# Scan tables of a two-layer trunk: complex products in three double-width VectorE steps, parameters of both layers made together early in layer 0

## The chip, the cores and the metric

The kernel runs on one core of a Trainium2 chip. The metric is the device time of one execution in microseconds (us); the median of several executions stands for a kernel. The engines are PE (TensorE, matrix products), DVE (VectorE), ACT (ScalarE), POOL (GpSimd) and SP (SyncE, which here issues most of the transfers). Each works through its own instructions in the order in which they were emitted, and waits at an instruction until what it needs is there.

## The reference, cut to what matters

The trunk has two layers over 256 latent and 256 context tokens of width 1024. Each layer mixes tokens through four parallel branches (multi-head latent attention, neighbourhood attention, an S5 scan, a Mamba-2 scan), merges them with gates, projects the sum, and then runs a mixture of 16 experts. The change concerns the S5 branch alone:

```python
def s5_scan(abar, bbar, u, h0, reverse):
    bu = jnp.einsum('gpc,btgc->btgp', bbar, u.astype(jnp.complex64))
    a = jnp.broadcast_to(abar, bu.shape)
    a_cum, h = lax.associative_scan(_linear_combine, (a, bu), reverse=reverse, axis=1)
    return h + a_cum * h0[:, None]
...
    for d, rev in ((0, False), (1, True)):
        a = lax.complex(a_re[d].astype(f32), a_im[d].astype(f32))
        abar = jnp.exp(jnp.exp(log_step[d].astype(f32))[:, None] * a)
        bbar = ((abar - 1.0) / a)[:, :, None] * lax.complex(b_re[d].astype(f32), b_im[d].astype(f32))
        cm = lax.complex(c_re[d].astype(f32), c_im[d].astype(f32))
        h_ctx = s5_scan(abar, bbar, uc, h_zero, rev)
        h_lat = s5_scan(abar, bbar, ul, h_ctx[:, 0] if rev else h_ctx[:, -1], rev)
        y_lat = y_lat + readout(cm, h_lat)
```

`abar`, `bbar` and `cm` depend on weights alone. The kernel turns them into tables: powers of `abar` times `bbar` (the input table), `cm` times powers of `abar` (the readout table), a kernel of short convolutions made from both, and powers of the rotation of `abar` over longer distances. The scan itself then consists of matrix products with these tables.

## The kernel before

The class `Trunk` runs `mix_phase` (L860) and then the expert phase, for layer 0 and then for layer 1. All products of activations and weights go through PE with each operand split in two parts (high and low), which makes three matmuls of each (L256 to L258). A weight arrives in `unit` (L361): SP issues the transfer into a slot of a ring `w` (two slots in the token mixing of layer 0), ACT makes the high part `wh` (L341), and DVE, for some units POOL, makes the low part `wl` (L342). SP issues in order, so a transfer whose slot is not free holds back those behind it.

Two streams of work are woven into the branches. `ada` (L446 to L474) makes the modulation of later stages from conditioning weights: SP loads tiles `wa` (four slots), PE multiplies (L454), DVE adds into `R` (L458), PE transposes `R` (L466). `merge` makes the gates and the merged stream `yT` (DVE at L1512 or L1521 and L1522, behind PE's products).

The tables of a layer are made in `s5_tables` (L690), a generator whose steps are emitted in turn with steps of `merge` by `together` (L938): for layer 0 in layer 0's token mixing after the neighbourhood attention, for layer 1 also in layer 0, after the S5 branch, just ahead of the projection. All of it happens in the first third of the run. The tables go to DRAM and are read back by the branch.

`s5_tables` first makes the parameters of its layer from 128x16 arrays: loads of `a` and the step sizes on ACT's queue, an exact exponential (`exp_exact`, L311), cosine and sine, nine powers `pw`, the factor `f`, and eight squarings `ro` of the rotation. Then for each half `h` of the groups: `bb` (128x128 twice), the input table `IT` in two parts of 128x4x128, each with real and imaginary part, the readout table `CP` in two parts of 128x4x144, PE transposes of `IT` (L822), a block diagonal `BD`, the PE products of `CP` and `BD` (L837), their copies `Kc`, and six doublings of `W` from 128x8 to 128x256 columns. The temporary tiles are named `t5...`, those of a complex product `cm1` to `cm4`.

Every complex product goes through `cmul` (L666): DVE makes four of the six steps (L683 to L686), POOL the other two (L687 and L688), the second of which needs DVE's L686.

What sets the order around the change is the order of emission, sorted by priorities: `first()` and `urgent()` raise the transfers and the splits of weights.

Of the kernel before, what the change touches and what calls it, by code (L numbers as in the profile page):

```python
# [12 lines left out]
F32 = mybir.dt.float32  # L13
# [3 lines left out]
OP = mybir.AluOpType  # L17
# [4 lines left out]
DEPTH = 2  # L22
# [168 lines left out]
class Trunk:  # L191
# [477 lines left out]
    def cmul(self, ore, oim, ar, ai, br, bi, shape, tag, pool, conj=False, im=None):  # L669

        nc = self.nc
        n = int(np.prod(shape))
        ar2, ai2 = im or (ar, ai)

        def tmp(s):
            x = self.sb([128, n], f"cm{s}", F32, pool)
            names = "abcd"[:len(shape)]
            if len(shape) == 1:
                return x
            return x.rearrange("p (" + " ".join(names) + ") -> p " + " ".join(names), **dict(zip(names, shape)))  # L680

        t1, t2, t3, t4 = tmp(1), tmp(2), tmp(3), tmp(4)
# [7 lines left out]
    def s5_tables(self, l):  # L690

        nc, t, wk = self.nc, self.t, self.ar
        dr = self.dr
        dt = lambda s, shape: dr.tile(shape, F32, name=f"s5{s}{l}", tag=f"s5{s}{l}")
        T = self.tabs[l] = {
            "IN": dt("in", [2, 128, 16 * 128]), "CP": dt("cp", [2, 128, 2 * 8 * 9 * 16]),
            "K": dt("k", [256, 240]), "W": dt("w", [2, 128, 2 * 8 * 64]),
            "R": dt("r", [128, 16]),
        }
        v = lambda s, shape=(128, 16): self.sb(list(shape), "t5" + s, pool=wk)  # L700
        a = v("a", (128, 2, 16))
        nc.scalar.dma_start(a, t["s5a"][l])
        x0 = v("x0")
# [12 lines left out]
        k, r, sn, sh, cm1, cs = v("k"), v("r"), v("sn"), v("sh"), v("cm1"), v("cs")  # L716
# [11 lines left out]

        pw = v("pw", (128, 2, 9, 16))
# [5 lines left out]
        def cm(o, i, j, b, tag):  # L735
            n = j - i
            bb = [pw[:, z, b, :][:, None, :].to_broadcast([128, n, 16]) for z in (0, 1)]
            self.cmul(pw[:, 0, o:o + n, :], pw[:, 1, o:o + n, :], pw[:, 0, i:j, :], pw[:, 1, i:j, :],
                      bb[0], bb[1], (n, 16), tag, wk)
        cm(2, 1, 2, 1, "p1")  # L740
        cm(3, 1, 3, 2, "p2")
        cm(5, 1, 5, 4, "p4")

        nre, f, dn, q1, q2 = v("nre"), v("f", (128, 2, 16)), v("dn"), v("q1"), v("q2")
# [10 lines left out]
        nc.vector.tensor_mul(f[:, 0, :], q1, dn)  # L755
# [9 lines left out]
        nc.scalar.dma_start(T["R"], R8)  # L765
        ro = v("ro", (128, 2, 9, 16))
        nc.vector.tensor_copy(ro[:, 0, 0, :], cs)
        nc.vector.tensor_copy(ro[:, 1, 0, :], sn)
        yield
        for j in range(1, 9):  # L770
            a_ = [ro[:, z, j - 1, :] for z in (0, 1)]
            self.cmul(ro[:, 0, j, :], ro[:, 1, j, :], a_[0], a_[1], a_[0], a_[1], (16,), "ro", wk)

        yield
        for h in range(2):
            qs = slice(h * 8, h * 8 + 8)
            b = v("b", (128, 2, 8, 16))
            c = v("c", (128, 2, 8, 16))
            nc.scalar.dma_start(b, t["s5b"][l, h])
            nc.scalar.dma_start(c, t["s5c"][l, h])  # L780
            cn = v("cn", (128, 2, 8, 16))
            nc.vector.tensor_scalar(cn, c, -1.0, None, OP.mult)
            bb = v("bb", (128, 2, 8, 16))
            fb = [f[:, z, qs][:, :, None].to_broadcast([128, 8, 16]) for z in (0, 1)]
            self.cmul(bb[:, 0], bb[:, 1], b[:, 0], b[:, 1], fb[0], fb[1], (8, 16), "bb", wk)

            pq = v("pq", (128, 2, 8, 9))
            for z in range(2):
                nc.vector.tensor_copy(pq[:, z], pw[:, z, :, qs].rearrange("p k q -> p q k"))
            yield  # L790

            IT = [v(f"IT{z}", (128, 8, 128)) for z in (0, 1)]
            for d in range(2):
                dq = lambda z: z.rearrange("p (g d) x -> p g d x", d=2)[:, :, d, :]
                po = []
                for z in range(2):
                    p_ = dq(pq[:, z])
                    p_ = p_[:, :, 7::-1] if d == 0 else p_[:, :, 0:8]
                    po.append(p_[:, :, :, None].to_broadcast([128, 4, 8, 16]))
                o = [dq(IT[z]).rearrange("p g (s c) -> p g s c", s=8) for z in (0, 1)]  # L800
                bs = [dq(bb[:, z])[:, :, None, :].to_broadcast([128, 4, 8, 16]) for z in (0, 1)]
                self.cmul(o[0], o[1], bs[0], bs[1], po[0], po[1], (4, 8, 16), "it", wk)
                yield

            CP = v("CP", (128, 2, 8, 9, 16))
            for d in range(2):
                dq = lambda z: z.rearrange("p (g d) x -> p g d x", d=2)[:, :, d, :]
                po = []
                for z in range(2):
                    p_ = dq(pq[:, z])  # L810
                    p_ = p_[:, :, 8::-1] if d == 1 else p_
                    po.append(p_[:, :, :, None].to_broadcast([128, 4, 9, 16]))
                o = [CP[:, z].rearrange("p (g d) i c -> p g d i c", d=2)[:, :, d] for z in (0, 1)]
                cc = [dq(y[:, z])[:, :, None, :].to_broadcast([128, 4, 9, 16]) for y in (c, cn) for z in (0, 1)]
                self.cmul(o[0], o[1], cc[0], cc[1], po[0], po[1], (4, 9, 16), "cp", wk, im=cc[2:])
                yield
            IN = v("IN", (128, 16, 128))
            for q4 in range(4):
                ps = self.psum("sm")
                for j in range(4):  # L820
                    q, z = divmod(q4 * 4 + j, 2)
                    nc.tensor.transpose(ps[:, j * 128:(j + 1) * 128], IT[z][:, q, :], self.ident)  # L822
                self.copy(IN[:, q4 * 4:(q4 + 1) * 4, :].rearrange("p a b -> p (a b)"), ps, eng=self.on("IN"))
            nc.scalar.dma_start(T["IN"][h], IN.rearrange("p a b -> p (a b)"))
            nc.scalar.dma_start(T["CP"][h], CP.rearrange("p z q i c -> p (z q i c)"))

            BD = v("BD", (128, 2, 8, 32))
            nc.gpsimd.memset(BD, 0.0)
            for g2 in range(2):
                self.copy(BD[g2 * 64:(g2 + 1) * 64, :, :, g2 * 16:(g2 + 1) * 16], bb[g2 * 64:(g2 + 1) * 64], eng=self.on("BD"))  # L830
            yield
            ps = self.psum("sm")
            for d in range(2):
                for g in range(4):
                    q = g * 2 + d
                    for z in range(2):
                        nc.tensor.matmul(ps[g * 32:(g + 1) * 32, d * 128:(d + 1) * 128], BD[:, z, q, :],  # L837
                                         CP[:, z, q, d:d + 8, :].rearrange("p i c -> p (i c)"),
                                         start=z == 0, stop=z == 1, tile_position=(0, g * 32))
# [9 lines left out]
            W = v("W", (128, 2, 8, 64))  # L849
            nc.vector.memset(W[:, 0, :, 0:1], 1.0)  # L850
            nc.vector.memset(W[:, 1, :, 0:1], 0.0)
            for j in range(6):
                n = 1 << j
                rb = [ro[:, z, 3 + j, qs][:, :, None].to_broadcast([128, 8, n]) for z in (0, 1)]
                self.cmul(W[:, 0, :, n:2 * n], W[:, 1, :, n:2 * n], W[:, 0, :, 0:n], W[:, 1, :, 0:n],
                          rb[0], rb[1], (8, n), f"w{j}", wk)
# [4 lines left out]
    def mix_phase(self, l):  # L861
        nc, t, tc = self.nc, self.t, self.tc
        with ExitStack() as es:
# [4 lines left out]
            side = dict(e=front, side="right") if l else dict(e=front)  # L868
# [1242 lines left out]
```

## Time and profile before

| | us |
|---|---|
| median of 3 runs | 1989.41 |
| the 3 runs | 1983.79 to 1990.79 |
| the profiled execution | 1984.16 |
| its span in the profile | 1982.4 |
| PE busy in it | 1691.3 |
| VectorE busy in it | 854.3 |
| GpSimd busy in it | 347.7 |

The profile is of one execution. Its busy times are summed over a run whose stages differ: in layer 0 the token mixing lasts from 0 to about 640 us, then come the experts until about 1110 us, then the same for layer 1. So a share of the whole span says little; the stretches in which the tables are made have to be read by themselves.

### The profile page before, as it was taken

To read this page: it belongs to the slowest core of one execution; us is meant where nothing else is said; L and a number is where in the kernel's file an instruction comes from. 1 tells how busy PE (TensorE), PEld (TensorE's weight loads), DVE (VectorE), ACT (ScalarE), POOL (GpSimd) and SP (SyncE) were. 2 spreads that over 40 slices of the span, in tenths; PEclk is the share of its full clock that TensorE was granted. 3 is DMA by queue.
4 is the path that set the end of the run, shared out by engine and by line. 5 is a ranking of instruction groups with operands and counts; after the bars stand their busy time and mean duration, and the time that the engine had idled before them with its cause. 6 is when DMAs were issued, how large, how long until landed. Compare 5 with 4: busy or idle time off the path is not lost.

```text
span 1982.4 us, 28289 instructions
## 1 busy us (share of the span) xinstructions
PE 1691.3 (85%) x11294; PEld 1031.6 (52%) x11294; DVE 854.3 (43%) x1866; ACT 499.4 (25%) x982; POOL 347.7 (18%) x463
## 2 busy tenths in 40 slices
PE   6999988999889799999888879889897766766765
PEld 2676666666668543434232259868895432322322
DVE  2357698557896521212121156567974110100102
ACT  5422423322324311101010164344352110000001
POOL 3231154234450000000000051333500000000000
PEclk9999999999999899999999989999997886776777
DMA  8747367274248699999999843435568999999996
GB/s 286 256 164 240 107 226 263 91 224 149 89 170 318 259 407 419 419 420 420 419 419 420 359 171 106 117 99 169 182 241 333 421 420 419 420 420 420 420 419 264
DMA packets 106735, 574.04 MB, mean 290 GB/s; under 512 B 13580, under 2 KB 17484, under 8 KB 55404
## 3 DMA queue, kind: packets, MB, share of 16 engines
q1 hardware_dynamic: 95052, 533.77, 69.2%
q0 software_dynamic: 5616, 20.52, 3.4%
q10 hardware_dynamic: 5936, 17.95, 2.4%
q8 instruction: 89, 1.46, 0.3%
q14 instruction: 42, 0.34, 0.1%
HBM read 556.47 MB, written 15.71 MB: 289 GB/s over the span
## 4 chain that ended last, share of the span: by engine, by line
PE 49%; DMA 32%; DVE 12%; ACT 2%; issue 2%; POOL 2%; SPq 0%; DVEq 0%; ACTq 0%; POOLq 0%
DMA w<-in_w_down_dram 11%; DMA w<-in_w_gate_dram 9%; DMA w<-in_w_up_dram 9%; PE psmm L1945 8%; PE psmm L256 7%; PE psmm L258 6%; PE psmm L257 6%; PE psmm L1974 4%; PE psbg L454 2%; DVE wl L342 2%; PE pssm L1847 1%; DMA wa<-in_w_ada_dram 1%; PE pssm L1993 1%; PE pssm L1012 1%; PE pssm L257 1%
## 5 line engine op out<-in xcount | busy, mean ns | idle before, releaser
L1945 PE MATMUL psmm<-w,xs 128*32 128x256 f32 (+1 forms) x3072 | 406.8, 527 | 101.2 <-DMA w<-in_w_up_dram 52.9
L1945 PEld LDWEIGHTS psmm<-w,xs 128*32 128x32 f32 (+1 forms) x3072 | 140.7, 133 | 355.1 <-issue 176.8
L258 PE MATMUL psmm<-hT,wl 128*128 128x512 f32 (+1 forms) x672 | 237.9, 354 | 4.4 <-DVE wl L342 4.3
L256 PE MATMUL psmm<-hT,wh 128*128 128x512 f32 (+1 forms) x672 | 241.3, 359 | 0.2 <-ACT wh L341 0.2
L257 PE MATMUL psmm<-hT,wh 128*128 128x512 f32 (+1 forms) x672 | 237.1, 353 | 0.0
L1974 PE MATMUL psmm<-w,aT 128*32 128x256 f32 (+1 forms) x1536 | 202.4, 521 | 37.3 <-DMA w<-in_w_down_dram 23.5
L341 ACT ACTIVATE wh<-w 128x1024 fp32r<-128x1024 f32 (+1 forms) x128 | 144.8, 1137 | 184.9 <-PE psmm L258 51.4
L342 DVE TENSOR_TENSOR wl<-w,wh 128x1024 fp32r<-128x1024 f32 (+1 forms) x101 | 139.7, 1390 | 55.7 <-ACT wh L341 55.5
L1974 PEld LDWEIGHTS psmm<-w,aT 128*32 128x32 f32 (+1 forms) x1536 | 69.4, 134 | 161.3 <-issue 80.4
L256 PEld LDWEIGHTS psmm<-hT,wh 128*128 128x128 f32 x672 | 128.3, 191 | 41.5 <-issue 20.6
L258 PEld LDWEIGHTS psmm<-hT,wl 128*128 128x128 f32 x672 | 128.2, 191 | 22.5 <-DVE wl L342 5.0
L257 PEld LDWEIGHTS psmm<-hT,wh 128*128 128x128 f32 x672 | 128.5, 191 | 18.2 <-issue 2.2
L244 DVE COPY YS<-psmm 32x512 f32<-32x512 f32 (+1 forms) x64 | 35.7, 558 | 234.6 <-PE psmm L1974 234.1
L1953 DVE SCALAR_TENSOR_TENSOR th<-th,psmm 128x512 f32<-128x512 f32 (+1 forms) x32 | 17.7, 555 | 225.5 <-ACT th L1952 225.5
L1954 DVE TENSOR_TENSOR th<-th,psmm 128x512 f32<-128x512 f32 (+1 forms) x32 | 17.7, 555 | 224.0 <-PE psmm L1945 224.0
L1804 POOL COPY sel<-cst 32x128 f32<-32x128 f32 (+1 forms) x24 | 6.8, 284 | 611.3 <-DVE GT L1812 576.4
L236 ACT ACTIVATE YS<-psmm 32x512 f32<-32x512 f32 (+1 forms) x64 | 30.7, 479 | 322.9 <-PE psmm L1974 322.4
L342 POOL TENSOR_TENSOR wl<-w,wh 128x1024 fp32r<-128x1024 f32 (+1 forms) x27 | 69.8, 2586 | 233.0 <-ACT wh L341 212.4
L258 PE MATMUL psmm<-wh,hT 128*128 128x256 f32 x288 | 83.6, 292 | 5.0 <-POOL hT L584 4.5
L256 PE MATMUL psmm<-wh,hT 128*128 128x256 f32 x288 | 84.0, 292 | 1.8 <-ACT hT L582 1.8
L257 PE MATMUL psmm<-wl,hT 128*128 128x256 f32 x288 | 82.7, 288 | 0.0
L1952 ACT ACTIVATE th<-psmm 128x512 f32<-128x512 f32 (+1 forms) x32 | 15.7, 490 | 212.2 <-PE psmm L1945 212.2
(533 smaller groups left out, 2721.3 us busy)
## 6 DMA issues: line engine op xcount, KB each, us to landing
w<-in_w_gate_dram SPq DMA_DIRECT2D x128, 1024.0 KB, 19.9
w<-in_w_up_dram SPq DMA_DIRECT2D x128, 1024.0 KB, 19.9
w<-in_w_down_dram SPq DMA_DIRECT2D x128, 1024.0 KB, 19.9
wa<-in_w_ada_dram SPq DMA_DIRECT2D x96, 512.0 KB, 5.8
w<-in_w_gb_dram SPq DMA_DIRECT2D x48, 640.0 KB, 4.2
w<-in_w_in_dram SPq DMA_DIRECT2D x40, 512.0 KB, 3.7
w<-in_w_gb_dram SPq DMA_DIRECT2D x20, 512.0 KB, 4.3
w<-in_w_out_dram SPq DMA_DIRECT2D x20, 512.0 KB, 5.0
```

The lines of the kernel that those rows point to most:

```text
L236: nc.scalar.activation(out, in_, AF.Copy)
L244: nc.vector.tensor_copy(out, in_)
L256: nc.tensor.matmul(out, lh, rh, start=start, stop=False)
L257: nc.tensor.matmul(out, lh, rl, start=False, stop=False)
L258: nc.tensor.matmul(out, ll, rh, start=False, stop=stop)
L341: nc.scalar.activation(hi, x, AF.Copy)
L342: (eng or nc.vector).tensor_tensor(lo, x, hi.bitcast(F32), OP.subtract)
L454: nc.tensor.matmul(ps[q:q + 32, :], self.sc[:, k].rearrange("p a b -> p (a b)"), w[:, j * 512:(j + 1) * 512], start=k == 0, stop=k == 7, t ...
L1012: nc.tensor.matmul(ps[:, :nk * 128], q(h, tt), k(h, nk * 128), start=True, stop=True)
L1847: nc.tensor.matmul(ps[:, kk, s, :n], self.x[2 * s + i][:, (k + kk) * 128:(k + kk + 1) * 128], oh[:, s, i], start=i == 0, stop=i == 1)
L1945: nc.tensor.matmul(ps[j * M:(j + 1) * M, :N], xs[:, k, e4].rearrange("p s c -> p (s c)"), w[:, kk, j * N:(j + 1) * N], start=n + kk == 0, ...
L1974: nc.tensor.matmul(bank(j)[j * M:(j + 1) * M, :N], aT[:, b, hf, :], w[:, kk, j * N:(j + 1) * N], start=k == 0, stop=k == 7, tile_position= ...
```

## The change

A new generator `tables_begin` makes the parameters of both layers at once, as arrays of 128x32. Its loads stand on SP's queue, and its steps are emitted right after `start`, which makes the first normalised activations `hT` of layer 0. Powers, rotations and the factor stay in SBUF in tiles `pw`, `ro` and `fb` of the pool `ap`.

`cmul` gives way to `product`: three DVE steps over real and imaginary part together (two products and a sum), so that `IT` and `CP` are made in steps of 128x1024 and 128x1152 columns. The operands for it, with negated and doubled parts, are made by copies on ACT, and the first part of `c` is loaded a second time. POOL keeps only the memset of `BD`.

```diff
-    def cmul(self, ore, oim, ar, ai, br, bi, shape, tag, pool, conj=False, im=None):
...
-        nc.vector.tensor_tensor(t1, ar, br, OP.mult)
-        nc.vector.tensor_tensor(t2, ai, bi, OP.mult)
-        nc.vector.tensor_tensor(ore, t1, t2, OP.add if conj else OP.subtract)
-        nc.vector.tensor_tensor(t3, ar2, bi, OP.mult)
-        nc.gpsimd.tensor_tensor(t4, ai2, br, OP.mult)
-        nc.gpsimd.tensor_tensor(oim, t4, t3, OP.subtract if conj else OP.add)
...
+    def tables_begin(self, es):
...
+        n = 16 * DEPTH
...
+        self.pw = self.ap.tile([128, 2, 9, n], F32, name="t5pw")
+        self.ro = self.ap.tile([128, 2, 6, n], F32, name="t5ro")
+        self.fb = self.ap.tile([128, 2, n], F32, name="t5f")
...
+        yield
+        nc.sync.dma_start(a.rearrange("p z (l q) -> p z l q", l=DEPTH), t["s5a"].rearrange("l p z q -> p z l q"))
         for g2 in range(2):
-            nc.scalar.dma_start(x0[g2 * 64:(g2 + 1) * 64, :], t["s5ls"][l, g2].partition_broadcast(64))
-        step = self.exp_exact(x0, 16, wk)
+            nc.sync.dma_start(x0[g2 * 64:(g2 + 1) * 64, :].rearrange("p (l q) -> p l q", l=DEPTH),
+                                t["s5ls"][:, g2].partition_broadcast(64))
+        step = self.exp_exact(x0, n, wk)
...
+    def product(self, out, a, b, tmp):
+
+        nc = self.nc
+        nc.vector.tensor_tensor(out, a[0], b[0], OP.mult)
+        nc.vector.tensor_tensor(tmp, a[1], b[1], OP.mult)
+        nc.vector.tensor_tensor(out, out, tmp, OP.add)
...
+            nc.scalar.dma_start(c[:, 0:2], t["s5c"][l, h])
+            nc.scalar.dma_start(c[:, 2], t["s5c"][l, h][:, 0])
+
+            self.copy(c[:, 1:3], c[:, 1:3], scale=-1.0, eng="act")
...
+            self.copy(bb[:, 0], bb[:, 2], scale=-1.0, eng="act")
...
+                self.product(dq(IT, d).rearrange("p q (s c) -> p q s c", s=8), bs, p_, tm()[:, :, 0:8])
                 yield
...
+                self.product(dq(CP, d).rearrange("p q (i c) -> p q i c", c=16), cc, p_, tm())
                 yield
...
+                begun = ExitStack()
+                begin = self.tables_begin(begun)
+                next(begin)
                 arena(self.start, hT)
+                for _ in begin:
+                    pass
+                begun.close()
```

On DVE's queue early in the run, between the last low parts of `hT` (L584) and the convolution blocks of the Mamba-2 branch (`cvu`, `cv`; L1165 and L1169, after the change L1177 and L1181), there stands before the change one split of a weight:

```order
48 L584 TENSOR_TENSOR hT_0_90<-hf_375,hT_0_89 128x256
49 L584 TENSOR_TENSOR hT_0_90<-hf_379,hT_0_89 128x256
50 L342 TENSOR_TENSOR wl_606<-w_603,wh_605 128x1024
51 L1165 SCALAR_TENSOR_TENSOR cvu_548<-psmm_523,cwh_504,cvu_548 128x2x254
52 L1165 SCALAR_TENSOR_TENSOR cvu_548<-psmm_523,cwh_504,cvu_548 128x2x255 x2
53 L1169 SCALAR_TENSOR_TENSOR cv_506<-cvt_553,cvu_548 128x512
```

After it, the last `hT` is row 63, and rows 64 to 141 lie between it and the first `cvu`. Here are the last of them:

```order
136 L761 TENSOR_TENSOR t5ro<-t5ca_117_532 128x32
137 L760 TENSOR_TENSOR t5ro<-t5ca_117_532,t5q_100_454 128x32
138 L758 TENSOR_TENSOR t5ca_118_537<-t5ro 128x64
139 L759 TENSOR_TENSOR t5q_100_454<-t5ro 128x32
140 L761 TENSOR_TENSOR t5ro<-t5ca_118_537 128x32
141 L760 TENSOR_TENSOR t5ro<-t5ca_118_537,t5q_100_454 128x32
142 L1177 SCALAR_TENSOR_TENSOR cvu_707<-psmm_682,cwh_663,cvu_707 128x2x254
```

77 steps of the parameters and one split (row 83) moved in between the activations and the first convolution block. A further 13 parameter steps stand ahead of the last `hT`, at rows 47 to 59.

On SP's queue in the same place, the loads of the parameters moved in behind the second unit of the input projection. Before:

```order
19 L368 DMA w_447<-in_w_in_dram 128x1024
20 L368 DMA w_517<-in_w_in_dram 128x1024
21 L901 DMA cstm_91<-in_cstm_dram 128x844
22 L446 DMA wa_509<-in_w_ada_dram 128x1024
23 L368 DMA w_564<-in_w_in_dram 128x1024
```

After:

```order
20 L368 DMA w_676<-in_w_in_dram 128x1024
21 L689 DMA t5a_126<-in_s5a_dram 128x4x16
22 L691 DMA t5x_6_127<-in_s5ls_dram 64x2x16 x2
23 L913 DMA cstm_91<-in_cstm_dram 128x844
24 L368 DMA w_723<-in_w_in_dram 128x1024
25 L446 DMA wa_668<-in_w_ada_dram 128x1024
26 L368 DMA w_762<-in_w_in_dram 128x1024
```

Three small transfers went in, and a unit `w` now stands ahead of the first tile `wa`.

On DVE's queue in the first table stretch, the step that adds into `R` (L458), for which PE waits, stands before the change behind the products for `IT` and some of those for `CP`:

```order
358 L683 TENSOR_TENSOR cm_502_2480<-t5bb_2373,t5pq_2384 128x512
359 L684 TENSOR_TENSOR cm_503_2481<-t5bb_2373,t5pq_2384 128x512
360 L342 TENSOR_TENSOR wl_2700<-w_2697,wh_2699 128x1024
361 L685 TENSOR_TENSOR t5IT_490_2428<-cm_502_2480,cm_503_2481 128x4x128
362 L686 TENSOR_TENSOR cm_515_2533<-t5cn_2371,t5pq_2384 128x576
363 L683 TENSOR_TENSOR cm_513_2531<-t5c_2368,t5pq_2384 128x576
364 L684 TENSOR_TENSOR cm_514_2532<-t5c_2368,t5pq_2384 128x576
365 L458 TENSOR_TENSOR R_1620<-R_1620,psbg_1621 128x512
```

After it, it stands behind both products for `IT` (rows 345 to 348, 351 and 353), both for `CP` (the last step is row 364), and the first doublings of `W`:

```order
364 L768 TENSOR_TENSOR t5CP_2397<-t5CP_2397,t5tm_2442 128x8x144
365 L768 TENSOR_TENSOR t5W_2616<-t5W_2616,t5tw_2619 128x16x2
366 L768 TENSOR_TENSOR t5bb_2669<-t5bb_2669,t5tb_2670 128x256
367 L766 TENSOR_TENSOR t5W_2616<-t5W_2616,t5ro 128x16x4
368 L767 TENSOR_TENSOR t5tw_2627<-t5W_2616,t5rn_2272 128x16x4
369 L342 TENSOR_TENSOR wl_2684<-w_2681,wh_2683 128x1024
370 L768 TENSOR_TENSOR t5W_2616<-t5W_2616,t5tw_2627 128x16x4
371 L766 TENSOR_TENSOR t5W_2616<-t5W_2616,t5ro 128x16x8
372 L767 TENSOR_TENSOR t5tw_2631<-t5W_2616,t5rn_2272 128x16x8
373 L458 TENSOR_TENSOR R_1779<-R_1779,psbg_1780 128x512
```

No step of the parameters stands in this stretch any more; the tables' first step comes right behind the tail of the neighbourhood attention, at row 340.

## Rows read from the trace of the kernel before

**Rows 1.** The page: busy time by engine; shares of the chain that ended last.
```profile
PE 1691.3 (85%) x11294; PEld 1031.6 (52%) x11294; DVE 854.3 (43%) x1866; ACT 499.4 (25%) x982; POOL 347.7 (18%) x463
...
PE 49%; DMA 32%; DVE 12%; ACT 2%; issue 2%; POOL 2%; SPq 0%; DVEq 0%; ACTq 0%; POOLq 0%
```

**Rows 2.** Busy time by stretch: us, PE, PEld, DVE, ACT, POOL, PEclk, DMA share, GB/s.
```profile
50.00:100.00 50.00, 49.23 (x239) 32.72 (x238) 19.66 (x25) 20.95 (x31) 14.43 (x8) 1.00 0.74 258
240.00:263.00 23.00, 23.00 (x121) 15.36 (x118) 16.70 (x107) 8.45 (x13) 6.71 (x23) 1.00 0.55 173
263.00:327.00 64.00, 51.01 (x337) 38.39 (x336) 59.73 (x115) 14.58 (x21) 39.91 (x44) 0.89 0.63 222
498.00:522.00 24.00, 24.00 (x108) 18.90 (x103) 20.50 (x113) 10.01 (x14) 7.81 (x24) 1.00 0.33 107
522.00:592.00 70.00, 54.74 (x283) 40.83 (x283) 67.65 (x121) 15.91 (x24) 45.20 (x46) 0.98 0.38 139
700.00:1100.00 400.00, 368.66 (x1765) 142.24 (x1764) 76.11 (x132) 51.53 (x102) 3.98 (x14) 1.00 1.01 418
```

**Rows 3.** PE's waits from 263 to 327, longest groups: waiter, releaser, total, times, longest.
```profile
PE psbg L466 <- DVE R L458: 6.7, 1, 6.7
PE pssm L822 <- POOL t5IT L688: 2.7, 1, 2.7
PE pssm L822 <- DVE t5IT L685: 1.8, 1, 1.8
```

**Rows 4.** PE's waits from 522 to 592, the longest groups.
```profile
PE pssm L822 <- DVE t5IT L685: 5.7, 4, 2.5
PE pssm L837 <- DVE t5CP L685: 3.2, 3, 2.0
PE pssm L822 <- POOL t5IT L688: 3.2, 4, 0.8
```

**Rows 5.** Groups by line and shape from 263 to 327 (busy us, mean ns | idle before).
```profile
L684 DVE TENSOR_TENSOR cm<-t5bb,t5pq 128x512 f32<-128x512 f32 x4 | 4.7, 1170 | 0.0
...
L683 DVE TENSOR_TENSOR cm<-t5bb,t5pq 128x512 f32<-128x512 f32 x4 | 3.8, 954 | 0.0
...
L685 DVE TENSOR_TENSOR t5IT<-cm,cm 128x512 f32<-128x512 f32 x4 | 3.6, 898 | 0.0
...
L686 DVE TENSOR_TENSOR cm<-t5bb,t5pq 128x512 f32<-128x512 f32 x4 | 2.7, 685 | 2.3 <-POOL t5IT L688 2.3
...
L688 POOL TENSOR_TENSOR t5IT<-cm,cm 128x512 f32<-128x512 f32 x4 | 8.4, 2097 | 7.8 <-DVE cm L686 6.3 <-ACT wh L341 1.3
```

**Rows 6.** The same view from 498 to 592: readout table and one parameter step.
```profile
L683 DVE TENSOR_TENSOR cm<-t5c,t5pq 128x576 f32<-128x576 f32 x4 | 6.4, 1602 | 0.0
...
L685 DVE TENSOR_TENSOR t5CP<-cm,cm 128x576 f32<-128x576 f32 x4 | 3.0, 748 | 0.0
...
L684 DVE TENSOR_TENSOR cm<-t5ro 128x16 f32<-128x16 f32 x8 | 1.4, 173 | 0.5
```

**Rows 7.** Two stretches behind PE's waits, columns as in group 2.
```profile
279.00:286.00 7.00, 7.00 (x38) 5.88 (x40) 7.00 (x11) 2.62 (x5) 2.75 (x3) 0.77 0.27 98
306.20:313.00 6.80, 6.80 (x45) 5.91 (x47) 5.65 (x6) 1.88 (x3) 6.54 (x4) 0.75 0.09 37
```

**Rows 8.** DVE's timeline from 40 to 80: start us, us, instruction, idle before.
```profile
52.23 1.76 DVE L584 TENSOR_TENSOR hT<-hf,hT 128x256 fp32r<-128x256 f32 x1 [2.88 <-ACT hf L238]
...
56.16 0.43 DVE L584 TENSOR_TENSOR hT<-hf,hT 128x256 fp32r<-128x256 f32 x1 [0.56 <-ACT hf L238]
63.09 1.23 DVE L342 TENSOR_TENSOR wl<-w,wh 128x1024 fp32r<-128x1024 f32 x1 [6.50 <-ACT wh L341]
65.39 2.31 DVE L1165 SCALAR_TENSOR_TENSOR cvu<-psmm,cwh,cvu 128x508 f32<-128x508 f32 x3 [1.08 <-ACT cvu L238]
```

**Rows 9.** DVE's timeline from 238 to 266: the first computed step of the parameters.
```profile
242.98 0.17 DVE L748 TENSOR_TENSOR t5q<-t5a 128x16 f32<-128x16 f32 x1
```

**Rows 10.** SP's timeline near the end of the token mixing: weights of the first expert.
```profile
629.73 2.01 SPq L1827 DMA_DIRECT2D w<-in_w_up_dram  x4
```

More of the change, by code (lines that the diff above doesn't have):

```diff
@@ L690, in s5_tables @@
[L690 to L703, printed above, removed]
+    def tables_begin(self, es):
+        nc, t, dr = self.nc, self.t, self.dr
+        n = 16 * DEPTH
+        for l in range(DEPTH):
+            dt = lambda s, shape: dr.tile(shape, F32, name=f"s5{s}{l}", tag=f"s5{s}{l}")
+            self.tabs[l] = {
+                "IN": dt("in", [2, 128, 16 * 128]), "CP": dt("cp", [2, 128, 2 * 8 * 9 * 16]),
+                "K": dt("k", [256, 240]), "W": dt("w", [2, 128, 2 * 8 * 64]),
+                "R": dt("r", [128, 16]),
+            }
+        self.pw = self.ap.tile([128, 2, 9, n], F32, name="t5pw")
+        self.ro = self.ap.tile([128, 2, 6, n], F32, name="t5ro")
+        self.fb = self.ap.tile([128, 2, n], F32, name="t5f")
+        wk = es.enter_context(self.tc.tile_pool(name="t5", bufs=1, side="right", reuse_waits="tile"))
+        v = lambda s, shape=(128, n): self.sb(list(shape), "t5" + s, pool=wk)
+        a, x0 = v("a", (128, 2, n)), v("x0")
+        yield
+        nc.sync.dma_start(a.rearrange("p z (l q) -> p z l q", l=DEPTH), t["s5a"].rearrange("l p z q -> p z l q"))
@@ L764, in s5_tables @@
         nc.vector.tensor_mul(R8, R8, R8)
-        nc.scalar.dma_start(T["R"], R8)
-        ro = v("ro", (128, 2, 9, 16))
+        for l in range(DEPTH):
+            nc.scalar.dma_start(self.tabs[l]["R"], R8[:, l * 16:(l + 1) * 16])
+        ro = v("ro", (128, 2, 3, n))
         nc.vector.tensor_copy(ro[:, 0, 0, :], cs)
         nc.vector.tensor_copy(ro[:, 1, 0, :], sn)
[L769 to L772, printed above, removed]
@@ L774, in s5_tables @@
-        yield
+        at = [ro[:, :, j, :] for j in range(3)] + [self.ro[:, :, j, :] for j in range(6)]
+        for a_, o in zip(at, at[1:]):
+            t1 = v("ca2", (128, 2, n))
+            nc.vector.tensor_tensor(t1, a_, a_[:, 0:1, :].to_broadcast([128, 2, n]), OP.mult)
+            nc.vector.tensor_mul(q2, a_[:, 1, :], a_[:, 1, :])
+            nc.vector.tensor_sub(o[:, 0, :], t1[:, 0, :], q2)
+            nc.vector.tensor_add(o[:, 1, :], t1[:, 1, :], t1[:, 1, :])
+    def product(self, out, a, b, tmp):
[3 more added lines that the diff above has]
+        nc.vector.tensor_tensor(out, out, tmp, OP.add)
@@ L793, in s5_tables @@
+            dq = lambda x, d: x.rearrange("p z q k -> p (z q) k")[:, d::2, :]
+            tm = lambda: v("tm", (128, 8, 9, 16))
             for d in range(2):
[L794 to L800, printed above, removed]
@@ L801, in s5_tables @@
[L801 to L802 removed]
+                p_ = [dq(pq[:, z], d) for z in range(2)]
+                p_ = [(x[:, :, 7::-1] if d == 0 else x[:, :, 0:8])[:, :, :, None].to_broadcast([128, 8, 8, 16]) for x in p_]
+                bs = [dq(bb[:, y:y + 2], d)[:, :, None, :].to_broadcast([128, 8, 8, 16]) for y in (1, 0)]
+                self.product(dq(IT, d).rearrange("p q (s c) -> p q s c", s=8), bs, p_, tm()[:, :, 0:8])
@@ L803, in s5_tables @@
                 yield
-            CP = v("CP", (128, 2, 8, 9, 16))
+            CP = v("CP", (128, 2, 8, 144))
             for d in range(2):
[L807 to L815, printed above, removed]
+                p_ = [dq(pq[:, z], d) for z in range(2)]
+                p_ = [(x[:, :, 8::-1] if d == 1 else x)[:, :, :, None].to_broadcast([128, 8, 9, 16]) for x in p_]
+                cc = [dq(c[:, y:y + 2], d)[:, :, None, :].to_broadcast([128, 8, 9, 16]) for y in (0, 1)]
+                self.product(dq(CP, d).rearrange("p q (i c) -> p q i c", c=16), cc, p_, tm())
@@ L852, in s5_tables @@
             for j in range(6):
[L853 to L856, printed above, removed]
+                m = 1 << j
+                rb = (self.ro[:, 0, j, qs][:, None, :, None].to_broadcast([128, 2, 8, m]),
+                      rn[:, :, j, :][:, :, :, None].to_broadcast([128, 2, 8, m]))
+                tw = v("tw", (128, 2, 8, 32))[:, :, :, 0:m]
+                self.product(W[:, :, :, m:2 * m], (W[:, :, :, 0:m], W[:, ::-1, :, 0:m]), rb, tw)
             nc.scalar.dma_start(T["W"][h], W.rearrange("p z q k -> p (z q k)"))
```

74 lines of the change are left out of this document (36 added, 38 removed).

## The prediction

> **What bounds the kernel now.** I read the page first: PE is busy 1691 of 1982 us and holds half of the chain that ended last, VectorE 854 and 12% [rows 1]. By these shares a change on VectorE looks idle. The stretches say otherwise. From 50 to 100 PE is busy 49.2 of 50 us: there VectorE has 30 us to spare. From 240 to 263 and from 498 to 522, where the parameters of the two tables are made, PE does not pause. From 263 to 327 and from 522 to 592, where the tables themselves are made, VectorE is busy 59.7 of 64 and 67.7 of 70 us, and PE stands still for 64.00 - 51.01 = 13.0 and 70.00 - 54.74 = 15.3 us [rows 2]. PE's waits name the cause: the step of `R` that queues behind the products on VectorE (6.7 us), the input table from VectorE and POOL (1.8 and 2.7 us), and in the second stretch the same tables again, in many pieces [rows 3, 4]. So VectorE bounds these two stretches and PE nearly all that lies around them.
>
> Does a gain there reach the end? The experts' transfers fill the DMA engines from 700 to 1100 (share 1.01) [rows 2], but their weights go through ring slots that the token mixing frees: those of the first expert are issued at 629.7, between the last units of the projection [rows 10]. What the token mixing saves, the start of this stream gains. I carry every microsecond to the end.
>
> **The products.** Before, an input product is four VectorE steps of 128x512. The step that runs while POOL is idle takes 0.685 us, the three others 0.954, 1.170 and 0.898; POOL's own last step takes 2.10 us, and VectorE waits 2.3 us for it in all [rows 5]. Together 14.8 us for four products. After, a product is three steps of 128x1024. Such a step, a weight split with nothing on POOL beside it, takes 1.23 us [rows 8]: four products are 12 x 1.23 = 14.8 us. VectorE gains nothing in busy time here; what it gains is the wait and POOL's part of the chain. The readout table: a step of 128x576 takes 0.748 us undisturbed, and the first of the product's steps 1.60 on average [rows 6]. From 0.685 at 512 and 1.23 at 1024 columns each column adds 1.06 ns, so 128x1152 is about 1.37, and 12 steps 16.4 us. With 2 x 3 steps for `bb`, 36 for `W` and the copies `Kc` I get some 42 to 45 us of table work per layer. The splits of weights and the merged stream, which run beside POOL too, shorten by some 3 to 5 us in each stretch.
>
> The copies that now prepare operands stand on ACT, which is busy 14.6 of 64 and 15.9 of 70 us [rows 2]: 10 or so small copies per half hide there, and if that cover is gone each costs VectorE its own length, under half a microsecond. The second load of `c` hides as the first does.
>
> **The parameters leave both stretches.** In the first, VectorE starts them at 243.0 [rows 9] and the tables at about 263: PE is fully busy meanwhile, so the 14 us of VectorE work that go do not themselves shorten anything, but the tables start 20 us earlier. In the second they fill VectorE between 498 and 522, with the tables right behind. Together VectorE is relieved of over 20 us in each stretch, while PE has only 13.0 and 15.3 us of standstill there: PE becomes the bound, and the standstill is the ceiling of the gain.
>
> **First stretch.** I walked through the new orders with durations of the rows. The input table is done at about 257, ahead of PE's transposes. One wait is left: the step of `R` now stands behind both tables' products and part of `W`. From 243: 6 x 1.23 (input), 6 x 1.37 (readout), 4 splits at 1.23, 6 `bb` steps at 0.41 (by the same slope), 12 small ones at 0.2, in all 25.4 us, less some overlap of neighbours: 266 to 268. PE gets there at about 263.5, so 3.5 us stay. Gain 13.0 - 3.5 = 9.5 us.
>
> **Second stretch.** The copies for `c` and `bb` stand on ACT behind the gates, which delays the first product, but not PE; about 1 us of wait is left. Gain 15.3 - 1 = 14.3 us.
>
> **Clock.** Behind two of the waits PE ran at a granted clock of 0.77 over 7 us and 0.75 over 6.8 us [rows 7], so at the lower level (1.2 GHz) for 3.2 and 3.4 us, of which half is lost: 1.6 and 1.7 us. PE stood still before both. The second of these waits goes, the first shrinks. I take 2 us, with bounds 0 and 4.
>
> **The early cost.** The parameters of both layers now stand early on VectorE: 77 steps between the last `hT` and the first convolution block. Before, that gap lasts from 56.6 to 65.4, with one split of 1.23 us in it [rows 8]: 7.5 us are free. 77 steps at 0.173 us, the price of a small step [rows 6], are 13.3 us, and two round trips to ACT come on top: the block is late by about 6.5 us. A block takes VectorE some 3 us of every 7, so it catches up within two. What PE loses in between is bounded below by nothing, or a gain of 1 if a late load of `wa` costs less than now, and above by the whole delay and the wait for a tile `wa` that stands on SP behind a unit whose slot is freed by the split in this block: 9 us. My walk has PE reach five tiles of `ada` in a row with four slots and wait 3 to 8 us, some of which it wins back when those tiles are not needed later. I take 4. The three small loads on SP's queue ahead of the next units cost that queue about 1 us, hidden behind slots that are not free anyway.
>
> Here the row that speaks against the early place is an `hT` step of 1.76 us where its twin takes 0.43 [rows 8], with POOL at work beside it: up to 1.3 us for one meeting. POOL is busy 14.4 us of the 50 [rows 2], and the dearest price is that it stops VectorE several times on the way through the parameters. The Trainium skill ("SBUF — State Buffer", section "SBUF: two separate sides") says that VectorE steps with two SBUF inputs and GpSimd share a port pair as an exclusive lock held for a whole instruction. By that rule a parameter step that meets a POOL split would wait up to that split's whole length, some 2 us, and the early cost would rise from 4 to 6 or 8 us; by the row the excess is 1.3 us at a time, and for the table steps of [rows 5], 0.2 to 0.5 us on average. The sum stays with the row.
>
> **The sum.** 1984.2 (profiled execution) - 9.5 - 14.3 - 2 + 4 = 1962.4, a gain of 21.8 us. That execution is 5.2 us below the median of the three runs, which spread over 7 us; their mean is 1988.0. From there the forecast is 1988.0 - 21.8 = 1966.
>
> **Rivals.**
> 1. The early block is dear: the late convolution and the `wa` tiles cost PE 9 us and POOL's splits stop VectorE three times by 1.3 us: 13 instead of 4, so 1975. For it: PE has no slack there [rows 2]. Against: VectorE has 30 us, and most blocks catch up.
> 2. The gain is swallowed: PE no longer waits for tables, but for the next thing, the units of weights through two ring slots and the order of merge and tables, and half to two thirds of the 23.8 us stay as other waits. With the early cost of 4, the time is 1980 to 1988. For it: the splits share VectorE's queue with longer steps, so one that comes up behind a product waits 1.4 us instead of 0.7. Against: the parameters' 14 us are gone from both stretches whatever the products do, and the products no longer wait for another engine.
> 3. Slower: it isn't POOL that stretches the steps, so the wide ones keep the price per column of now. Input: 14.8 us for 16 x 512 columns, 1.81 ns each, so 12 x 1024 columns cost 22.2 (+7.4); the readout table and `W` in proportion, together 44 us of busy table work now (59.7 less some 16 us of other steps) x 1.5 = 66, +18 per layer after 4 us of waits on POOL that go. In the first stretch the earlier start of 20 us pays for it, but the step of `R` comes some 9 us later than I walked, and PE loses about what it loses now; in the second +18 - 14 = +4; with an early cost of 9 the time is 1988 + 4 + 9 = 2001. It decides from a mean of about 1.7 us for a 128x1024 step. Against it: 0.685 and 0.748 us are rows of the same operation in the same stretch, with POOL idle. A split of that very width takes 1.23 us [rows 8].
>
> **Chances.** The forecast (1953 to 1976) 0.58; the early block dear (1972 to 1980) 0.14; swallowed 0.16; slower 0.12. What a measurement of this kernel can tell from no change is about 0.5%, 10 us: faster means below 1979.5. That gives faster 0.70, within 0.5% 0.18, slower 0.12. The range from 1953 (no early cost, all standstill and clock regained: 1988 - 28.3 - 4 = 1956, less the spread of the runs) to 1986 holds 0.8.
>
> **What would show it.** Right: PE busy over 60 of 64 us at 250 to 315, with one wait left on `R`; no wait on the input table in the second stretch; wide steps at 1.2 to 1.4 us; the first expert's weights issued some 20 us earlier than 629.7. Wrong: waits of PE on `wa` or on the convolution's banks of over 8 us before 100; wide steps over 1.7 us; new waits for `wl` or a `gt` in the two stretches; a gain at 630 that is gone at 1100.

## The result, and the profile after

The changed kernel takes 1964.13 us (median of 4 runs, 1960.38 to 1966.83) against 1987.54 (4 runs, 1983.79 to 1990.79) for the kernel before: ratio 0.9882, 95% interval 0.9855 to 0.9908. The gain is 23 us where 21.8 were forecast, and the median is 2 us below the predicted 1966. Two further measurements beside other kernels gave 0.9889 (0.9863 to 0.9915) and 0.9885 (0.9867 to 0.9902).

The page of the changed kernel, busy time by engine (to [rows 1]):

```profile
PE 1694.7 (86%) x11294; PEld 1034.4 (53%) x11294; DVE 830.7 (42%) x1716; ACT 503.6 (26%) x1008; POOL 252.5 (13%) x331
```

PE's work is what it was; VectorE has 24 us less of it, POOL 95. By stretch (columns as in [rows 2], the same three clock times):

```profile
50.00:100.00 50.00, 46.15 (x218) 30.58 (x218) 34.12 (x111) 20.32 (x31) 14.05 (x8) 0.97 0.76 240
...
263.00:327.00 64.00, 62.26 (x391) 45.73 (x390) 50.19 (x86) 17.30 (x28) 1.67 (x3) 0.97 0.82 294
...
522.00:592.00 70.00, 67.61 (x356) 55.29 (x355) 58.28 (x102) 24.72 (x45) 3.55 (x2) 0.95 0.57 205
```

In both table stretches PE is now busy over 96%, VectorE 78 and 83% instead of 93 and 97%. Early, PE has lost 3 us. PE's wait for tiles `wa` before 240 (0.8 us in the kernel before), then all its waits from 240 to 327, then from 498 to 592 (to [rows 3, 4]):

```profile
PE psbg L454 <- DMA wa<-in_w_ada_dram: 3.7, 2, 3.2
...
PE psbg L454 <- DMA wa<-in_w_ada_dram: 1.7, 1, 1.7
...
PE psmm L256 <- ACT wh L341: 1.3, 1, 1.3
PE psmm L257 <- DVE wl L342: 1.1, 1, 1.1
PE pssm L827 <- DVE gt L1533: 0.8, 1, 0.8
```

No wait on a table and none on `R` is left in these stretches. The wide steps, from 498 to 592 (to [rows 5, 6]):

```profile
L767 DVE TENSOR_TENSOR t5tm<-t5c,t5pq 128x1152 f32<-128x1152 f32 x4 | 5.4, 1356 | 0.0
...
L766 DVE TENSOR_TENSOR t5IT<-t5bb,t5pq 128x1024 f32<-128x1024 f32 x4 | 4.9, 1221 | 0.0
```

A clock time does not mean the same work in two kernels. So I cut both runs where the same instruction starts: the first score maximum of the neighbourhood attention (L1015), the first scan instruction of the S5 branch (L1405), the last step of `yT` (L1522). These are the three stretches, the kernel before first, then the changed one:

```profile
0.00:205.60 205.60, 180.31 (x1052) 123.81 (x1054) 96.31 (x212) 73.96 (x122) 59.26 (x68) 1.00 0.70 234
205.60:444.48 238.88, 224.22 (x1219) 151.81 (x1216) 171.62 (x438) 80.69 (x167) 80.55 (x100) 0.97 0.54 184
444.48:604.01 159.53, 142.16 (x754) 105.26 (x754) 132.14 (x297) 43.26 (x67) 76.20 (x99) 0.98 0.41 137
```

```profile
0.00:213.23 213.23, 185.59 (x1052) 126.84 (x1054) 113.23 (x306) 77.16 (x128) 58.96 (x68) 0.98 0.70 226
213.23:440.06 226.83, 223.69 (x1219) 150.18 (x1216) 153.15 (x316) 80.62 (x177) 33.16 (x34) 0.99 0.56 194
440.06:581.13 141.07, 138.07 (x754) 104.72 (x754) 111.91 (x175) 43.83 (x77) 28.11 (x33) 0.98 0.46 156
```

The three L numbers are those of the kernel before; in the changed one they are 12 higher. PE has the same number of entries in each (1052, 1219, 754). The head is 7.6 us longer, the first table stretch 12.1 shorter, the second 18.5 shorter: 22.9 us at the end of the merge. PE's standstill (length less busy) goes from 25.3 to 27.6, from 14.7 to 3.1, from 17.4 to 3.0. The first expert's `w_up` follows:

```profile
607.26 1.40 SPq L1839 DMA_DIRECT2D w<-in_w_up_dram  x3
```

That is 22.5 us ahead of [rows 10]. Layer 0's experts keep the gain: PE's first product of their outputs `YS` (L1993) comes 23.4 us ahead.

In layer 1 part of it is lost, far from the tables. From the last scan of its S5 branch to its last `yT`, this profile takes 53.95 us where the kernel before takes 48.62. VectorE makes the same steps of `Hb` in the same order, but one of them meets a weight split on GpSimd. Here is that step with the split and with PE's wait behind it, and then the same step in the kernel before:

```profile
1410.79 3.79 DVE L1437 TENSOR_TENSOR Hb<-s5t,s5t 64x124 f32<-64x124 f32 x1
...
1411.56 2.87 POOL L342 TENSOR_TENSOR wl<-w,wh 128x1280 fp32r<-128x1280 f32 x1
...
PE pssm L1450 <- DVE Hb L1439: 3.2, 1, 3.2
```

```profile
1433.94 0.54 DVE L1425 TENSOR_TENSOR Hb<-s5t,s5t 64x124 f32<-64x124 f32 x1
```

In the kernel before the split falls on a step of `yT` instead, and PE does not wait. All three profiles of the changed kernel have this wait of 3.2 us, and the stretch takes 53.95, 54.07 and 52.50 us in them. At the last `YS` they are 17.7, 17.2 and 24.7 us ahead. Two of the experiments below (the parameters in the gaps of `start`, two early splits on VectorE) do not have the wait, though they too have the new products and the early parameters. So it hangs on how the queues happen to meet, and whether every execution of the changed kernel has it isn't known. The profiled executions are 17.3 us apart, the medians 23.

### The profile page after: what moved, and what is told of

Same layout as the page of the kernel before. It is cut to its first block, busy times and chain, and to the rows that moved or that the text cites. A ratio compares the mean times of both kernels' runs of the same rounds, so it can differ in the third digit from the quotient of the medians.

```text
span 1965.1 us, 27931 instructions
## 1 busy us (share of the span) xinstructions
PE 1694.7 (86%) x11294; PEld 1034.4 (53%) x11294; DVE 830.7 (42%) x1716; ACT 503.6 (26%) x1008; POOL 252.5 (13%) x331
## 5 line engine op out<-in xcount | busy, mean ns | idle before, releaser
L1965 DVE SCALAR_TENSOR_TENSOR th<-th,psmm 128x512 f32<-128x512 f32 (+1 forms) x32 | 17.7, 554 | 225.6 <-ACT th L1964 225.6
L1966 DVE TENSOR_TENSOR th<-th,psmm 128x512 f32<-128x512 f32 (+1 forms) x32 | 17.7, 554 | 217.8 <-PE psmm L1957 217.8
```

The lines of the kernel that those rows point to most:

```text
L1965: nc.vector.scalar_tensor_tensor(th, th, 1.0, pg[:, :N], OP.add, OP.mult)
L1966: nc.vector.tensor_tensor(th, th, pu[:, :N], OP.mult)
```

## The experiments

Each kernel was timed beside the kernel before. "Head", "first" and "second" are the stretches above, cut at the same instructions; PE's standstill is in brackets.

| kernel | ratio (95% interval) | head | first | second |
|---|---|---|---|---|
| before | 1 | 205.6 (25.3) | 238.9 (14.7) | 159.5 (17.4) |
| the change | 0.9882 (0.9855 to 0.9908) | 213.2 (27.6) | 226.8 (3.1) | 141.1 (3.0) |
| parameters early, old products | 1.0035 (1.0017 to 1.0053) | 211.1 (28.8) | 241.2 (15.9) | 157.9 (15.5) |
| new products alone | 0.9930 (0.9908 to 0.9953) | 208.2 (26.7) | 233.8 (10.2) | 142.0 (3.8) |
| change + GpSimd work | 1.0023 (1.0001 to 1.0044) | 210.7 (27.2) | 238.3 (10.7) | 156.5 (15.1) |
| parameters early, six narrow steps on VectorE | 0.9911 (0.9881 to 0.9940) | 213.3 (28.2) | 232.8 (6.4) | 139.6 (2.5) |

### Parameters early, products as before

```diff
-    def product(self, out, a, b, tmp):
+    def cmul(self, ore, oim, ar, ai, br, bi, shape, tag, pool, conj=False, im=None):
+        ...          (the six steps of the kernel before, two of them on GpSimd)
```

> Of the change only the early parameters of both layers; the products stay as before, in narrow steps on VectorE and GpSimd. Theory A (TensorE's standstill of 13.0 and 15.3 us is the ceiling, and either half of the change lifts most of it): the early cost stays (the first convolution block about 9 us late, about 7 us lost by 200), the first table stretch gains 10, the second 12, so 1970 to 1976 us. Rival B (the products on GpSimd are the cause by themselves): VectorE stays over 90% busy in both stretches, the waits of TensorE on the tables stay above 15 us in all, and with the early cost the time is 1982 to 1990.

1991.95 us against 1985.13: ratio 1.0035, a third of a per cent slower. Theory A falls. Rival B is the nearer: PE stands still for 15.9 and 15.5 us, though the time is above B's range too, and VectorE's share is 82% from 263 to 327. Here are the window from 522 to 592, PE's longest wait in the first stretch, and the costliest narrow step in the second:

```profile
522.00:592.00 70.00, 58.30 (x293) 45.17 (x294) 64.40 (x118) 19.48 (x28) 39.62 (x43) 0.93 0.46 155
```

```profile
PE psbg L466 <- DVE R L458: 9.6, 1, 9.6
```

```profile
L778 DVE TENSOR_TENSOR cm<-t5bb,t5pq 128x512 f32<-128x512 f32 x4 | 6.6, 1649 | 0.0
```

The tables no longer wait for parameters, and PE waits as long as before. The step of `R` stands at its new place behind more table steps, and these still run beside GpSimd, at a mean of up to 1.65 us where 0.69 is the undisturbed price. VectorE is still busy 92% of the second window.

### The products alone

```diff
-        qs = slice(l * 16 + h * 8, l * 16 + h * 8 + 8)
+        qs = slice(h * 8, h * 8 + 8)     (parameters 128x16 per layer, made at their old places)
```

> Of the change only the products in three wide steps on VectorE; the parameters are made layer by layer at their old places. Theory A: no early cost; the parameters still hold the start of the tables back by 20 us, so the wait on R and the first input table stays (about 6 us in the first stretch, 3 in the second), the later waits go: gain 14 to 17, 1971 to 1974 us. Rival B (the wide products alone are the gain): 1962 to 1966. Rival C (the parameters are the gain): 1982 to 1988.

1969.40 us, ratio 0.9930, and a second time 1968.43, 0.9906 (0.9889 to 0.9924). The products alone bring 16 to 18 of the 23 us. That is A's gain of 14 to 17 or 1 us more (as a time 2 to 3 us below A's range, and 2 to 3 above B's), but A's ground (either half lifts most) is gone. The second stretch is as short as with the whole change (142.0 against 141.1 us), with the parameters still in it. Only the first keeps 7 us of standstill more, and not where A expected it: PE waits neither for `R` nor for a table, but 5.9 us for `P` of the neighbourhood attention (1.4 with the whole change) and 3.8 for `wa` tiles (1.7). Why `P` is later here was not followed.

### The whole change, with GpSimd work put back

Here GpSimd makes products that nobody uses.

```diff
+        if noise:
+            for _ in range(2):
+                nc.gpsimd.tensor_tensor(self.noise[2], self.noise[0], self.noise[1], OP.mult)
```

> The whole change, and in addition two GpSimd products of 128x512 on constant tiles behind each wide product of the input and readout tables; nobody waits for them. Theory A (GpSimd's work beside them is what stretched VectorE's steps before): the wide steps of 1.22 and 1.35 us grow to 1.6 to 2.0 on average, VectorE's time in each stretch rises by 10 to 17 us, TensorE waits again for 2 to 6 us in each, 1968 to 1976 us. Rival F (the steps were long for another reason): the steps stay within 5% and the time at 1962 to 1966.

1988.81 us: the whole gain is gone, more than A expected. The first steps of the input table beside GpSimd, GpSimd's products, and PE's waits, all in the first stretch:

```profile
L766 DVE TENSOR_TENSOR t5IT<-t5bb,t5pq 128x1024 f32<-128x1024 f32 x4 | 7.1, 1768 | 0.0
```

```profile
L771 POOL TENSOR_TENSOR nz<-nz,nz 128x512 f32<-128x512 f32 x16 | 28.8, 1802 | 1.2
```

```profile
PE pssm L833 <- DVE t5IT L768: 4.3, 1, 4.3
PE psbg L466 <- DVE R L458: 3.7, 1, 3.7
```

VectorE's busy time rises from 153.2 to 166.9 and from 111.9 to 125.8 us in the two stretches, 27.7 us in all, for some 58 us of GpSimd products (28.8 in these sixteen, 29.0 in the sixteen of the second stretch). GpSimd's steps are stretched too: the shortest takes 1.27 us, the mean is 1.81. Nothing waits for that work, so its length is no part of any chain: it costs because it stretches VectorE's steps, for which PE waits.

### Six narrow steps, all on VectorE

```diff
-        nc.gpsimd.tensor_tensor(t4, ai2, br, OP.mult)
-        nc.gpsimd.tensor_tensor(oim, t4, t3, OP.subtract if conj else OP.add)
+        nc.vector.tensor_tensor(t4, ai2, br, OP.mult)
+        nc.vector.tensor_tensor(oim, t4, t3, OP.subtract if conj else OP.add)
```

> Parameters early, and the products in six narrow steps as before, but all six on VectorE. Theory G (what gained is that GpSimd no longer works beside the tables and in their chain; the width is a detail): six steps at 0.69 and 0.75 us are 4.1 and 4.5 us per product against 3.66 and 4.05 in three wide ones, so VectorE has some 4 to 6 us more per layer than in the changed kernel, which TensorE's cover takes: 1963 to 1970 us. Rival H (the width itself is the gain): the time stays near that with GpSimd, 1980 to 1992.

1969.16 us, ratio 0.9911: theory G. Against the first experiment only the engine of two steps differs, and 1.2% lies between the two. From 498 to 592 every narrow step runs at its undisturbed price:

```profile
L777 DVE TENSOR_TENSOR cm<-t5bb,t5pq 128x512 f32<-128x512 f32 x4 | 2.7, 683 | 0.0
```

The most telling reading is VectorE's busy time in the two table stretches, 157.6 + 115.9 = 273.4 us with all six steps, and 159.4 + 119.4 = 278.8 us in the first experiment with four of the six. Work given to GpSimd took nothing off VectorE. Between this kernel and the change, timed beside it, lie 4 us (1969.16 against 1965.20). They hold the width and the copies that moved to ACT with it; the intervals overlap, so the width isn't shown to be worth anything.

### Other places for the parameters

```diff
+            for _ in self.begin:      (loads first of all, steps in the gaps of start)
+                pass
             for h in ada:
```

> The whole change, but the loads of the parameters are the first transfers, and their steps stand inside start, in the gaps that VectorE has from 4 to 43 us, not between hT and the convolution. Theory A (the early cost of the change comes from that block alone: a late first convolution block, 3.2 us of TensorE waiting for wa at 70, and clock drops behind it): the first cvu is back at 64 to 67 us, the wait at 70 is gone, and 5 to 7 us come back: 1957 to 1960. Rival D (the early loss is the new order of the ada tiles, not the block on VectorE): the loss by 200 stays at 5 us or more, 1963 to 1966. Rival E: the steps now delay hT by 3 us or more, and the time stays at 1963 to 1967.

1958.87 us, 0.9869 (0.9853 to 0.9885), which looked better; repeated beside the change it was 1964.48 against 1963.33 (0.9889 and 0.9885). The expectations for that pair:

> The changed kernel once more, side by side with the two that follow. All theories: 1962 to 1966 us, ratio 0.987 to 0.990.

> The products alone, parameters at their old places, once more. Theory G (without GpSimd beside the tables the parameters matter little): 3 to 6 us above the changed kernel, 1966 to 1971. Rival M (the early parameters are worth nothing at all): the two within 2 us of each other.

> The parameters in the gaps of start, once more. Theory N (that place is better than the one of the change, since TensorE neither waits for wa at 70 nor finds R late): 3 to 7 us below the changed kernel, 1957 to 1962. Rival O (the difference of the first measurement was between chips and executions): within 2 us of the changed kernel.

So rivals O and, in the trace, E: the wait of 3.2 us at 70 is gone, but the steps delay `hT`, and the first convolution block is still 6.6 us late (6.0 in the repeat). PE's time up to 54.5, against 35.91 of 54.50 us in the changed kernel:

```profile
0.00:54.50 54.50, 30.40 (x151) 13.80 (x152) 27.83 (x141) 26.51 (x49) 13.49 (x29) 0.97 0.73 251
```

The third place was ahead of the neighbourhood attention:

```diff
                 self.filler = m2
+                if l == 0:
+                    with ExitStack() as begun:
+                        for _ in self.tables_begin(begun):
+                            pass
                 arena(self.na, l)
```

> The whole change, but the parameters of both layers are made after the Mamba-2 branch, just ahead of the neighbourhood attention, where VectorE is busy some 27 of 40 us. Theory I (the block on VectorE between hT and the convolution is what costs 3 to 5 us by 205): the loss by 190 falls to 0 to 3 us, the tables start with all parameters made, and the time is 1957 to 1962. Rival J (the block costs as much wherever it stands, since VectorE steps that TensorE waits for queue behind it): 1962 to 1968.

1962.26 us (0.9877, 0.9850 to 0.9904), beside 1965.20 for the change (0.9889):

> The changed kernel again, as the measure for the others of this call. All theories: 1961 to 1967 us; by 205 us of the program it is 5 to 8 us behind the kernel before, at 700 it is 21 to 25 us ahead.

The first convolution block is on time here (+1.0 us), but at the cut behind the head this kernel is 8.4 us behind, with 26 more entries of PE moved ahead of that cut, so its head cannot be compared. At the end of the merge it is 23.6 us ahead, as the change is (23.3 in the profile taken beside it). By the time (0.3 us above Theory I's range) it is rival J, within the noise. The place of the parameters is not worth 5 us in any of the three.

### Who holds up the small steps

```diff
-            "low": (1, 0, 0, 1, 0, 1, 1, 0, ...
+            "low": (1, 0, 0, 0, 0, 0, 1, 0, ...     (two early weight splits from GpSimd to VectorE)
```

> The whole change, but the two weight splits that GpSimd makes while VectorE goes through the parameters (2.4 us each) are made by VectorE. Theory K (the two parameter steps of 2.41 and 2.38 us, whose like take 0.19, were held up by these splits): no small step above 0.5 us is left in the block, the first convolution block comes 1 to 3 us earlier (65.4 + 6.5 to 8.5), the time falls by 0 to 3 us. Rival L (something else holds those steps, or VectorE's 2 x 1.23 us cost as much): the long steps stay, or the block comes no earlier than 9 us late.

In the changed kernel VectorE's timeline in the early block has two small steps of over 2 us, and GpSimd's two weight splits at the same moments:

```profile
55.72 2.41 DVE L321 TENSOR_SCALAR xeu<-xet 128x32 f32<-128x32 f32 x1 [0.64 <-ACT xet L320]
...
66.15 2.38 DVE L739 TENSOR_TENSOR t5q<-t5q,t5q 128x32 f32<-128x32 f32 x1
...
74.89 2.31 DVE L1177 SCALAR_TENSOR_TENSOR cvu<-psmm,cwh,cvu 128x508 f32<-128x508 f32 x3
```

```profile
55.70 2.39 POOL L342 TENSOR_TENSOR wl<-w,wh 128x1024 fp32r<-128x1024 f32 x1 [2.23 <-DVE hT L584]
65.70 2.78 POOL L342 TENSOR_TENSOR wl<-w,wh 128x1024 fp32r<-128x1024 f32 x1 [7.61 <-ACT wh L341]
```

With these splits on VectorE the same two steps take 0.17 and 0.19 us, no small step in the block takes over 0.5 us, and the convolution comes 1.1 us earlier than in that profile (the change's other two have it at 75.35 and 74.00):

```profile
56.08 0.17 DVE L321 TENSOR_SCALAR xeu<-xet 128x32 f32<-128x32 f32 x1
...
67.16 0.19 DVE L739 TENSOR_TENSOR t5q<-t5q,t5q 128x32 f32<-128x32 f32 x1
...
68.63 0.49 DVE L727 TENSOR_TENSOR t5pw<-t5ca,t5cb 128x128 f32<-128x128 f32 x2
...
73.81 2.31 DVE L1177 SCALAR_TENSOR_TENSOR cvu<-psmm,cwh,cvu 128x508 f32<-128x508 f32 x3
```

Theory K on the cause. On the time it brought nothing (1965.76, ratio 0.9899, interval 0.9870 to 0.9928): PE now waits 7.3 us for `wa` tiles in the head instead of 3.7, and the head ends 11.0 us behind the kernel before.

```profile
PE psbg L454 <- DMA wa<-in_w_ada_dram: 7.3, 2, 5.0
```

## Why the prediction was right, step by step

**The bound.** Right in the main. PE's standstill in the two table stretches was named as the ceiling; 25.9 of its 32.0 us went, and PE is the bound now. In the second stretch it was not quite a ceiling: 18.5 us went, more than the 17.4 of standstill. The way to layer 0's experts was right too: `w_up` is issued 22.5 us earlier, and the first `w_gate` of the same expert, which the prediction did not read, at 580.34 instead of 603.22. That every microsecond reaches the end was not: each profile of the change loses 4 to 5 us again in layer 1, where the step of `Hb` meets a split.

**The price of a wide step.** Right: 1.22 and 1.35 us, where 1.23 and 1.37 were worked out from a split and a slope. Rival 3, dearer wide steps, is excluded, and the experiment with GpSimd work shows what it would have needed: the steps of the input table at 1.77 us on average and the gain gone, near the 1.7 that the rival named.

**Which half of the change gains.** Here the working was wrong, though the sum was not touched. It held that the parameters' 14 us are gone from both stretches "whatever the products do", and that the products give VectorE no busy time back beyond 3 to 5 us on other steps. The first experiment took 12.3 and 12.7 us of busy time off VectorE in the two stretches (171.6 to 159.4, 132.1 to 119.4), and PE's standstill hardly moved (32.0 to 31.4 in all). The second took 4.4 and 12.2 off and left 14.0, and brought 16 to 18 us. The step that failed is the one that set three free steps of 1.23 us against the four disturbed ones, saw 14.8 us on either side, and then counted the relief in VectorE's busy time. PE waits until `R` or a piece of a table is done. The prediction named GpSimd's part in that chain but gave it no price of its own, and with GpSimd still beside them the steps in it stayed long (up to 1.65 us), and the step of `R`, behind more of them, starts at 284.07 where the kernel before has it at 277.98, though the tables could begin earlier. The parameters add some 5 us on top of the products (1963.3 against 1968.4 side by side; the intervals of the two ratios, 0.9867 to 0.9902 and 0.9889 to 0.9924, overlap slightly), nearly all of it in the first stretch, 7 us shorter there, less the early cost.

**The early cost, forecast 4 us.** Mis-sized: 7.6 us at the end of the head, in this profile. Two terms were off. The first convolution block came 9.5 us late, not 6.5, since the two small steps met GpSimd splits and took 2.4 us each. There the row of 1.76 us, which the sum kept to, was the worse guide, and the rule of the Trainium skill ("SBUF — State Buffer", section "SBUF: two separate sides", a lock held for the whole instruction) the better: the trace agrees with it, 2.41 and 2.38 us beside splits of 2.39 and 2.78, and each step ends within 0.1 us of the split. That section of the Trainium skill names VectorE steps with two SBUF inputs or in a two-port mode; the first of the two held here has a single input, and no run shows in which mode it ran. The second term was not in the sum at all: 2.3 us of the 7.6 are standstill, and 5.3 us are PE's busy time for the same 1052 entries (180.3 to 185.6). The clock accounts for about that much: in the kernel before it is granted at 1.00 all through the head, after the change it is below that in three stretches (columns as in [rows 2]):

```profile
70.00:75.00 5.00, 4.84 (x15) 2.63 (x15) 4.69 (x34) 0.00 (x0) 0.00 (x0) 0.68 0.91 311
...
140.00:160.00 20.00, 19.18 (x99) 14.06 (x98) 10.65 (x28) 5.73 (x11) 11.45 (x17) 0.91 0.46 158
...
180.00:213.23 33.23, 30.61 (x189) 22.62 (x190) 17.99 (x38) 6.29 (x9) 4.92 (x6) 0.95 0.69 213
```

Their lengths times what is missing to 1.00 make 1.6 + 1.8 + 1.7 = 5.1 us. Only the first of the three stands right behind the wait of 3.2 us (67 to 70); its 0.68 is a mean between the two levels of 1.2 and 2.4 GHz. How firm is 7.6? Six profiles have this early block: they are 7.6, 7.2, 6.0, 5.4, 5.1 and 7.7 us behind at this cut (the change three times, the first, third and fourth experiment). The second experiment has none and was 2.6 and, repeated, 1.0 behind. The kernel with the two splits on VectorE, 11.0 behind, is left out, since it changes the block itself. Between the means, 6.5 and 1.8, the block costs near 5 us, and single profiles scatter by over 1 us on either side: the forecast of 4 is within that.

**The first stretch, forecast 9.5 and 2 for the clock.** Measured 12.1. The 3.5 us of waiting for `R` did not come, and that was luck: the step of `R` is done at 276.5, some 9 us later than walked, and PE reaches its transposes at 276.96, 13.5 us later than walked:

```profile
275.85 0.69 DVE L458 TENSOR_TENSOR R<-R,psbg 128x512 f32<-128x512 f32 x1
...
276.96 0.60 PE L466 MATMUL psbg<-cst,R 128*128 128x128 f32 x4
```

PE finds it ready by 0.4 us. 7.6 us of either delay are the longer head. What the walk had wrong in the rest was not followed up. The clock's 2 us do not show here: PE's busy time for the same 1219 entries fell by 0.5 us (224.2 to 223.7).

**The second stretch, forecast 14.3.** Measured 18.5: 14.4 of standstill as forecast, and 4 us less busy time of PE for the same 754 entries (142.2 to 138.1). The mean granted clock of the two is equal (0.98), so it isn't that. By line, the most of it lies in matmuls of the tables and of `ada` (by the lines of the kernel before, L822 5.3 to 4.5 us, L837 4.2 to 2.7, L454 6.3 to 5.3); why they are shorter stays open.

Taken as gains, the errors are -3.6 (early cost), +2.6 and +4.2 (the two stretches) and -2 (the clock's own term): together 1 us. So the total is better than its parts, by luck, and the 4 to 5 us lost in layer 1 of the profiles were in no term. Of the rivals' sums, the second's does not come out: half to two thirds of 23.8 us left as waits, with an early cost of 4, make 1980 to 1984, not 1988.

## What to carry to other kernels

Judge an engine by the stretch in which others wait for it, not by its share of the run: VectorE at 43% was the bound for some 130 us, and those were worth 23. Busy time alone does not tell what a relief is worth: 12 us less on VectorE in each stretch gained nothing as long as what PE waits for was as late as before. Work that is moved from VectorE to GpSimd as a relief has to be timed with VectorE's own steps beside it; here two of six steps on GpSimd left VectorE with no less busy time and PE with 31 us of standstill in the two table stretches. And two parts of a change that seem to relieve the same engine should be run apart before either is given the credit.

## What the runs showed of the hardware

A VectorE step of 128x32 that takes 0.19 us takes 2.4 us when it meets a GpSimd split of 2.4 us, and one of 64x124 takes 3.79 instead of 0.54 us beside a split of 2.87. All three end within 0.2 us of the end of the split. So the price of these meetings was what was left of the other instruction, not a share of the own length. About half of the GpSimd time put back in the third experiment came out as VectorE time (27.7 of 58 us). And the standstill of PE at 67 to 70 was followed by a lower clock: granted 0.68 on average from 70 to 75, where the kernel before, without that wait, had 1.00. Behind the wait for `Hb` it was 0.57 from 1415 to 1422.5.
